# First-layer modulation matmuls: two weight loads to a run, placed first among the ready work

## The chip, the cores and the metric

The kernel runs on one core of a Trainium2 chip. A core has five engines with a queue each: TensorE (PE in the profile) for matmuls, VectorE (DVE), ScalarE (ACT), GpSimd (POOL), and SyncE (SP), which here issues nearly all transfers. Matmuls read SBUF and write PSUM banks of 128 partitions by 2 KB; a bank is free again when another engine has copied it out, which the text calls an evacuation. The metric is the time of one execution on the device in microseconds (us).

## The reference

The reference is a two-layer transformer backbone with 256 context tokens and 256 latent tokens, model width 2048. Each layer first makes shift, scale and gate vectors for the latent and the context stream from a condition vector; the normalised tokens are scaled and shifted by them, and only then go into the wide input projection:

```python
for l in range(DEPTH):                       # DEPTH = 2, D_MODEL = 2048
    shift, scale, gate = jnp.split(sc @ w_ada[l] + b_ada[l], 3, axis=-1)
    shift_c, scale_c, gate_c = jnp.split(sc_ctx @ w_ada[l] + b_ada[l], 3, axis=-1)
    h_lat = rms_norm(x, norm_g[l]) * (1.0 + scale[:, None]) + shift[:, None]
    h_ctx = rms_norm(xc, norm_g[l]) * (1.0 + scale_c) + shift_c
    lat_a, lat_b = mixer_inputs(h_lat, w_in[l], ...)      # h @ w_in, then q, k, v, gates
    ...
```

Two attention groups (grouped-query and latent-compressed), gates, an output projection and a gated residual follow, and after the second layer a final norm. The change touches only `sc @ w_ada[0]` and `sc_ctx @ w_ada[0]`, the shift and scale columns of them, in the first layer.

## The kernel before

Everything is float32. A projection product is made of three matmuls (L141, L142, L143, helper `mm3`): each operand is split into a rounded part `hi` (ScalarE, L114) and the rest `lo` (VectorE or GpSimd, L116), and hi x hi, lo x hi, hi x lo are summed into one of four `acc` banks of PSUM. VectorE evacuates a full bank by adding it onto a tile in SBUF (L449; L453 for the first time).

The first layer cannot project before its tokens are modulated, and the modulation needs 32 MB of `w_ada`. So `layer0` cuts the 16 blocks of 128 model columns into seven parts (block edges 0, 1, 2, 4, 6, 8, 12, 16, so parts 0 to 6 of 128, 128, 256, 256, 256, 512 and 512 columns). While the projections (`kv`, `cb`, `q`, `g` in the tile names) run over the model rows of one part, the sums of the next part are made between them. `ada_pe` does that for one part, as a generator: it loads the part's weights in loads of 1 MB (`ra` tiles, L210; two loads for 128 columns, four for 256, eight for 512; scale columns first, then shift) and multiplies 16, 8 or 4 slices of 128 rows per load with a stationary operand of 32 columns (`scp`, which holds the latent and the context vector). The matmuls L225 go in turn to four groups of 32 partitions of an `att` bank; L235 copies the bank, the small matmuls L239 add up the four groups and turn the result, and `ada_store` (L197, L199) writes scale and shift. Then `modulated` writes the tokens of the next part: per block and stream L359 on VectorE (`xT`), one ScalarE operation, and L361 on VectorE (`h`).

`wtile`, which loads and splits each projection weight, steps the generator (`bg_step`) five times per call in this stage, so each `yield` is a place where projection work comes between. Parts 0 and 1 load ahead of their first matmul. The `ra` tiles come from a pool of 14 buffers that holds much else; four or five of them are in turn at `ra`'s disposal, and a load waits on SyncE's queue until the matmuls that read its buffer before have run. The order of all instructions on each engine is fixed when the kernel is built: a scheduler simulates the program and takes, for each engine, the ready instruction of the highest priority; without other marks that goes by the order of the code.

Of the kernel before, what the change touches and what calls it, by code (L numbers as in the profile page):

```python
# [48 lines left out]
class Net:  # L49
# [151 lines left out]
    def ada_pe(self, l, c0, w, ahead=False):  # L201

        nc = self.nc
        n = 2048 // w
        at = [(kind, m) for kind in (1, 0) for m in range(0, KT, n)]

        def load(kind, m):
            r = self.blk("ra").rearrange("p (k n) -> p k n", k=n)
            wa = self.a["w_ada0"][m * P : (m + n) * P, kind * D + c0 : kind * D + c0 + w]
            self.ra = nc.sync.dma_start(out=r, in_=wa.rearrange("(k p) n -> p k n", p=P))  # L210
            return r

        rs = {}
        if ahead:
            rs = {z: load(*z) for z in at}
            yield

        ps = self.bank("att")[:, :w]
        for kind, m in at:
            r = rs[kind, m] if ahead else load(kind, m)  # L220
            for i in range(n):
                g = i % 4
                o = 2 if kind else 0
                with self.after(None if c0 else self.order):
                    nc.tensor.matmul(  # L225
                        ps[32 * g : 32 * g + 32, :],
                        lhsT=self.scp[:, m + i, o : o + 32],
                        rhs=r[:, i, :],
                        start=kind == 1 and m + i < 4,
                        stop=kind == 0 and m + i >= 12,  # L230
                    )
            if (kind, m) != at[-1]:
                yield
        part = self.tmp("part")[:, :w]
        nc.scalar.copy(part, ps)  # L235
        n = w // P
        f = self.bank("att")[:, : 4 * n].rearrange("p (k v) -> p k v", k=n)
        for i in range(n):
            nc.tensor.matmul(f[:, i, :], lhsT=part[:, i * P : (i + 1) * P], rhs=self.sel, start=True, stop=True)  # L239
        for kind in (1, 0):  # L240
            o = 0 if kind else 2
            self.ada_store(l, kind, f[:, :, o : o + 2], c0)
        yield
# [950 lines left out]
```

## Time and profile before

| | us |
|---|---|
| median of 3 runs | 1425.3 (1422.45 to 1426.04) |
| the profiled execution | 1427.46 |
| its span, first to last instruction | 1425.5 |
| TensorE busy | 1344.1 (94% of the span) |
| VectorE busy | 1092.9 (77%) |
| ScalarE busy | 602.6 (42%) |
| GpSimd busy | 404.0 (28%) |

The profiled execution lies 2.16 us above the median, and its own time is 1.96 us more than its span; a sum made from its rows stands against 1427.46. The mean granted clock of TensorE over the span is 0.983 of full speed. A number like 0.39 behind the start of a projection matmul is its own duration; matmuls overlap, so how fast they follow each other is read from their starts. A float32 matmul that is not split (L225, L239) leaves two records in the trace.

### The profile page before, as it was taken

To read this page: it belongs to the slowest core of one execution; us is meant where nothing else is said; L and a number is where in the kernel's file an instruction comes from. 1 tells how busy PE (TensorE), PEld (TensorE's weight loads), DVE (VectorE), ACT (ScalarE), POOL (GpSimd) and SP (SyncE) were. 2 spreads that over 40 slices of the span, in tenths; PEclk is the share of its full clock that TensorE was granted. 3 is DMA by queue.
4 is the path that set the end of the run, shared out by engine and by line. 5 is a ranking of instruction groups with operands and counts; after the bars stand their busy time and mean duration, and the time that the engine had idled before them with its cause. 6 is when DMAs were issued, how large, how long until landed. Compare 5 with 4: busy or idle time off the path is not lost.

```text
span 1425.5 us, 21028 instructions
## 1 busy us (share of the span) xinstructions
PE 1344.1 (94%) x7516; PEld 1128.2 (79%) x7516; DVE 1092.9 (77%) x2297; ACT 602.6 (42%) x974; POOL 404.0 (28%) x385
## 2 busy tenths in 40 slices
PE   5999999998998999898998999999999999999996
PEld 4765687887786987787886778898898989888884
DVE  2775568899796999988999864976787776856566
ACT  4321223544443242355532234665555644454443
POOL 0110025423222230222222113543234431223335
PEclk8999999999999999999999999999999999999999
DMA  9976733455555666443567665655775757733444
GB/s 307 349 262 223 284 113 89 144 166 166 159 175 179 205 213 211 151 139 126 190 216 220 214 208 184 203 150 177 234 256 163 234 153 249 260 110 126 156 137 143
DMA packets 142120, 272.47 MB, mean 191 GB/s; under 512 B 8336, under 2 KB 53824, under 8 KB 140608
## 3 DMA queue, kind: packets, MB, share of 16 engines
q1 hardware_dynamic: 142016, 271.13, 59.2%
q8 instruction: 59, 0.97, 0.3%
q14 instruction: 45, 0.37, 0.1%
HBM read 264.78 MB, written 6.32 MB: 190 GB/s over the span
## 4 chain that ended last, share of the span: by engine, by line
PE 59%; DVE 18%; DMA 12%; issue 5%; ACT 3%; POOL 2%; SPq 1%; DVEq 0%; POOLq 0%; ACTq 0%
PE acc L141 17%; PE acc L143 17%; PE acc L142 16%; DMA rad<-in_w_adaT 8%; DVE junk L269 7%; DVE lo L116 5%; PE att L225 2%; PE att L588 2%; PE att L611 1%; DMA cb<-in_cr 1%; DVE sm L593 1%; DMA ra<-in_w_ada 1%; DVE pt L148 1%; DMA raw<-in_w_in 1%; ACT p L596 1%
## 5 line engine op out<-in xcount | busy, mean ns | idle before, releaser
L114 ACT CAST hi<-raw 128x1024 fp32r<-128x1024 f32 (+2 forms) x279 | 271.8, 977 | 395.8 <-PE acc L142 224.2
L116 DVE TENSOR_TENSOR lo<-raw,hi 128x512 fp32r<-128x512 f32 (+2 forms) x446 | 305.6, 726 | 89.5 <-PE acc L143 37.5
L116 POOL TENSOR_TENSOR lo<-raw,hi 128x512 fp32r<-128x512 f32 (+2 forms) x112 | 153.7, 1393 | 476.5 <-PE acc L143 367.4
L141 PE MATMUL acc<-hi,h 128*128 128x512 f32 (+1 forms) x672 | 240.6, 361 | 6.1 <-ACT cq L451 4.9
L142 PE MATMUL acc<-hi,h 128*128 128x512 f32 (+1 forms) x672 | 238.1, 357 | 0.0
L269 DVE CUSTOM_DVE_ANT_0 junk<-rad,cb 128x512 bf16<-128x512 f32 x224 | 176.9, 790 | 73.5 <-DMA rad<-in_w_adaT 46.8
L143 PE MATMUL acc<-lo,h 128*128 128x512 f32 (+1 forms) x672 | 226.7, 359 | 3.0 <-DVE lo L116 2.3
L269 DVE CUSTOM_DVE_ANT_0 junk<-rad,cb,as 128x512 bf16<-128x512 f32 x224 | 190.3, 849 | 3.8
L142 PE MATMUL acc<-h,lo 128*128 128x512 f32 (+1 forms) x512 | 171.5, 340 | 2.7 <-DVE lo L116 2.6
L143 PE MATMUL acc<-h,hi 128*128 128x512 f32 (+1 forms) x512 | 170.0, 338 | 0.0
L141 PE MATMUL acc<-h,hi 128*128 128x512 f32 (+1 forms) x512 | 165.7, 343 | 1.9 <-DVE g L453 1.2
L599 POOL TENSOR_SCALAR p<-p,sm 128x512 f32<-128x512 f32 (+1 forms) x96 | 85.7, 898 | 284.9 <-DVE sm L597 249.3
L143 PE MATMUL acc<-lo,y 128*128 128x512 f32 x384 | 146.2, 400 | 9.7 <-DVE lo L116 8.7
L141 PE MATMUL acc<-hi,y 128*128 128x512 f32 x384 | 151.0, 398 | 2.3 <-ACT y L147 1.9
L141 PEld LDWEIGHTS acc<-hi,h 128*128 128x128 f32 x672 | 127.3, 189 | 32.8 <-issue 5.8
L142 PE MATMUL acc<-hi,y 128*128 128x512 f32 x384 | 151.7, 395 | 0.2 <-DVE y L148 0.2
L143 PEld LDWEIGHTS acc<-lo,h 128*128 128x128 f32 x672 | 124.5, 189 | 22.7 <-DVE lo L116 3.9
L142 PEld LDWEIGHTS acc<-hi,h 128*128 128x128 f32 x672 | 127.2, 189 | 15.4
L141 PEld LDWEIGHTS acc<-h,hi 128*128 128x128 f32 x512 | 93.6, 190 | 18.0 <-issue 2.1
L142 PEld LDWEIGHTS acc<-h,lo 128*128 128x128 f32 x512 | 96.9, 190 | 12.8 <-DVE lo L116 3.7
L143 PEld LDWEIGHTS acc<-h,hi 128*128 128x128 f32 x512 | 96.7, 190 | 9.8
L143 PEld LDWEIGHTS acc<-lo,y 128*128 128x128 f32 x384 | 73.1, 191 | 28.4 <-DVE lo L116 12.6
(219 smaller groups left out, 2292.2 us busy)
## 6 DMA issues: line engine op xcount, KB each, us to landing
rad<-in_w_adaT SPq DMA_DIRECT2D x128, 512.0 KB, 4.5
raw<-in_w_in SPq DMA_DIRECT2D x125, 512.0 KB, 4.4
raw<-in_w_out SPq DMA_DIRECT2D x72, 512.0 KB, 4.1
ra<-in_w_ada SPq DMA_DIRECT2D x32, 1024.0 KB, 8.7
raw<-in_w_in SPq DMA_DIRECT2D x48, 288.0 KB, 3.0
raw<-in_w_ukv SPq DMA_DIRECT2D x16, 512.0 KB, 3.4
cb<-in_cr SPq DMA_DIRECT2D x6, 1024.0 KB, 7.1
raw<-in_w_uq SPq DMA_DIRECT2D x12, 512.0 KB, 3.7
```

The lines of the kernel that those rows point to most:

```text
L114: nc.scalar.copy(h, t)
L116: e.tensor_tensor(out=lo[:, c], in0=t[:, c], in1=fr(h[:, c]), op=ALU.subtract)
L141: mm(out, lhsT=ah, rhs=bh, start=first, stop=False)
L142: mm(out, lhsT=al, rhs=bh, start=False, stop=False)
L143: return mm(out, lhsT=ah, rhs=bl, start=False, stop=last)
L148: self.nc.vector.tensor_tensor(out=lo, in0=src, in1=fr(hi), op=ALU.subtract)
L225: nc.tensor.matmul(ps[32 * g : 32 * g + 32, :], lhsT=self.scp[:, m + i, o : o + 32], rhs=r[:, i, :], start=kind == 1 and m + i < 4, stop=k ...
L269: nc.vector.tensor_tensor_reduce(out=junk, in0=r[:, cs], in1=cb[:, v, cs], scale=1.0, scalar=o if i else 0.0, op0=ALU.mult, op1=ALU.add, a ...
L588: self.order = nc.tensor.matmul(banks[j], lhsT=q[:, qs], rhs=k[:, ks], start=i == 0, stop=i == len(score) - 1)
L593: nc.vector.tensor_reduce(out=nb[:, c], in_=v, axis=AX.X, op=ALU.max)
L596: nc.scalar.activation(pr[j], banks[j], AF.Exp, bias=nb[:, j : j + 1], scale=sc[:, j : j + 1], accum_out=l[:, j : j + 1])
L599: nc.gpsimd.tensor_scalar(out=pr[j], in0=pr[j], scalar1=l[:, j : j + 1], scalar2=1.0, op0=ALU.mult, op1=ALU.mult)
```

## The change

`ada_pe` now groups its loads in twos (`runs`). Both loads of a pair are issued, then the matmuls of the second load and those of the first are written one behind the other, under `high_priority`, which puts them ahead of other ready work in the scheduler's choice; the `yield` stands behind the pair. The flags for the first and the last matmul of each group of partitions follow the new order. From here on the lines stand 4 higher (L225 is L229, L239 is L243, L449 is L453).

```diff
+        runs = [at[i : i + 2] for i in range(0, len(at), 2)]
         rs = {}
         if ahead:
             rs = {z: load(*z) for z in at}
             yield
 
         ps = self.bank("att")[:, :w]
-        for kind, m in at:
-            r = rs[kind, m] if ahead else load(kind, m)
-            for i in range(n):
-                g = i % 4
-                o = 2 if kind else 0
-                with self.after(None if c0 else self.order):
-                    nc.tensor.matmul(
-                        ps[32 * g : 32 * g + 32, :],
-                        lhsT=self.scp[:, m + i, o : o + 32],
-                        rhs=r[:, i, :],
-                        start=kind == 1 and m + i < 4,
-                        stop=kind == 0 and m + i >= 12,
-                    )
-            if (kind, m) != at[-1]:
+
+        for run in runs:
+            if not ahead:
+                rs = {z: load(*z) for z in run}
+            for j, (kind, m) in enumerate(run[::-1]):
+                for i in range(n):
+                    g = i % 4
+                    o = 2 if kind else 0
+                    with self.after(None if c0 else self.order), self.tc.high_priority():
+                        nc.tensor.matmul(
+                            ps[32 * g : 32 * g + 32, :],
+                            lhsT=self.scp[:, m + i, o : o + 32],
+                            rhs=rs[kind, m][:, i, :],
+                            start=run is runs[0] and j == 0 and i < 4,
+                            stop=run is runs[-1] and j == 1 and i >= n - 4,
+                        )
+            if run is not runs[-1]:
                 yield
```

The number of instructions on each engine stays the same. In the fixed order, past some 190 us of the trace of before, the instructions of every engine follow each other as before; GpSimd's order is unchanged throughout.

TensorE's queue in part 5, before (`att_1036` is the bank of its sums, `ra_...` a load, `acc_...` a projection's bank; 32x512 x2 is two matmuls of 32 columns by 512):

```order
L141 MATMUL acc_974<-hi_953,h_667 128x512
L142 MATMUL acc_974<-hi_953,h_668 128x512
L143 MATMUL acc_974<-lo_954,h_667 128x512
L225 MATMUL att_1036<-ra_1049,scp 32x512
L141 MATMUL acc_982<-hi_953,h_667 128x512
L142 MATMUL acc_982<-hi_953,h_668 128x512
L143 MATMUL acc_982<-lo_954,h_667 128x512
```

and the same projection weights (`hi_953`) in the order of the change:

```order
L141 MATMUL acc_958<-hi_953,h_667 128x512
L142 MATMUL acc_958<-hi_953,h_668 128x512
L143 MATMUL acc_958<-lo_954,h_667 128x512
L141 MATMUL acc_966<-hi_953,h_667 128x512
L142 MATMUL acc_966<-hi_953,h_668 128x512
L229 MATMUL att_1036<-ra_1051,scp 32x512 x4
L229 MATMUL att_1036<-ra_1049,scp 32x512 x4
L143 MATMUL acc_966<-lo_954,h_667 128x512
```

Where one matmul of a load stood alone between two projection products, all four of it now stand behind the four of the load that comes after it, eight in a row.

TensorE's queue at the start, before: the sums of parts 0 (`att_199`) and 1 (`att_260`) and the first projection.

```order
L225 MATMUL att_199<-ra_194,scp 32x128 x16
L225 MATMUL att_199<-ra_196,scp 32x128 x16
L239 MATMUL att_234<-k,part_232 128x4
L225 MATMUL att_260<-ra_248,scp 32x128 x16
L225 MATMUL att_260<-ra_250,scp 32x128 x16
L141 MATMUL acc_300<-hi_255,h_239 128x512
```

and in the change:

```order
L229 MATMUL att_199<-ra_196,scp 32x128 x16
L229 MATMUL att_199<-ra_194,scp 32x128 x16
L243 MATMUL att_234<-k,part_232 128x4
L229 MATMUL att_260<-ra_250,scp 32x128 x16
L229 MATMUL att_260<-ra_248,scp 32x128 x16
L141 MATMUL acc_300<-hi_255,h_239 128x512
```

The two loads of each part have changed places; `ra_248` is still loaded ahead of `ra_250`.

VectorE's queue where the modulation for part 5's blocks is written, before (`kv`, `cb` and `q` are the tiles that projections are evacuated into):

```order
L449 TENSOR_TENSOR kv_252<-acc_1091,kv_252 128x512
L116 TENSOR_TENSOR lo_1195<-raw_1192,hi_1194 128x512 x2
L449 TENSOR_TENSOR cb_326<-acc_1134,cb_326 128x512
L449 TENSOR_TENSOR cb_326<-acc_1142,cb_326 128x512
L449 TENSOR_TENSOR cb_326<-acc_1150,cb_326 128x512
L197 TENSOR_TENSOR mod_88<-att_1126,vec_86 128x8
L197 TENSOR_TENSOR mod_87<-att_1126,vec_86 128x8
L199 SCALAR_TENSOR_TENSOR mod_88<-mod_88,vec_86 128x8
L359 SCALAR_TENSOR_TENSOR xT_99<-xT_99,mod_88,rb 128x256
L449 TENSOR_TENSOR cb_326<-acc_1158,cb_326 128x512
L359 SCALAR_TENSOR_TENSOR xT_99<-xT_99,mod_88,rb 128x256 x7
L449 TENSOR_TENSOR q_55_354<-acc_1199,q_55_354 128x512
```

and in the change:

```order
L197 TENSOR_TENSOR mod_88<-att_1087,vec_86 128x8
L197 TENSOR_TENSOR mod_87<-att_1087,vec_86 128x8
L199 SCALAR_TENSOR_TENSOR mod_88<-mod_88,vec_86 128x8
L363 SCALAR_TENSOR_TENSOR xT_99<-xT_99,mod_88,rb 128x256
L453 TENSOR_TENSOR kv_252<-acc_1111,kv_252 128x512
L363 SCALAR_TENSOR_TENSOR xT_99<-xT_99,mod_88,rb 128x256 x7
L365 SCALAR_TENSOR_TENSOR h_1128<-xT_99,mod_87,h_1127 128x256
L453 TENSOR_TENSOR kv_252<-acc_1119,kv_252 128x512
L116 TENSOR_TENSOR lo_1195<-raw_1192,hi_1194 128x512 x2
L453 TENSOR_TENSOR cb_326<-acc_1160,cb_326 128x512
L365 SCALAR_TENSOR_TENSOR h_1128<-xT_99,mod_87,h_1127 128x256 x4
L453 TENSOR_TENSOR cb_326<-acc_1168,cb_326 128x512
```

The same twenty-odd operations have moved ahead of the evacuations of one `kv` and all four `cb` accumulators and of the two casts `lo_1195`.

## Rows read from the trace of the kernel before

**Rows 1.** The page: busy time of an engine; the chain that ended last.

```profile
PE 1344.1 (94%) x7516; PEld 1128.2 (79%) x7516; DVE 1092.9 (77%) x2297; ACT 602.6 (42%) x974; POOL 404.0 (28%) x385
...
PE 59%; DVE 18%; DMA 12%; issue 5%; ACT 3%; POOL 2%; SPq 1%; DVEq 0%; POOLq 0%; ACTq 0%
PE acc L141 17%; PE acc L143 17%; PE acc L142 16%; DMA rad<-in_w_adaT 8%; DVE junk L269 7%; DVE lo L116 5%; PE att L225 2%; PE att L588 2%; PE att L611 1%; DMA cb<-in_cr 1%; DVE sm L593 1%; DMA ra<-in_w_ada 1%; DVE pt L148 1%; DMA raw<-in_w_in 1%; ACT p L596 1%
```

**Rows 2.** Windows: length, each engine's busy us, granted clock, DMA share, GB/s.

```profile
28.00:32.00 4.00, 1.56 (x36) 1.03 (x26) 0.64 (x2) 0.12 (x1) 0.00 (x0) 0.50 1.13 340
...
38.00:50.00 12.00, 12.00 (x58) 9.64 (x60) 10.30 (x22) 7.48 (x15) 1.43 (x2) 1.00 1.09 361
60.00:80.00 20.00, 20.00 (x134) 13.90 (x133) 19.74 (x38) 8.02 (x13) 6.66 (x8) 1.00 1.09 360
...
140.00:160.00 20.00, 19.61 (x99) 13.23 (x98) 16.93 (x33) 4.48 (x9) 2.73 (x2) 1.00 0.60 219
```

**Rows 3.** Timeline, TensorE, 26 to 36 us: start, duration, [idle before it <-releaser].

```profile
27.60 1.94 PE L225 MATMUL att<-ra,scp 128*32 128x128 f32 x32 [1.41 <-DMA ra<-in_w_ada]
31.98 1.93 PE L225 MATMUL att<-ra,scp 128*32 128x128 f32 x32 [2.44 <-DMA ra<-in_w_ada]
...
35.29 0.63 PE L142 MATMUL acc<-hi,h 128*128 128x512 f32 x1
35.71 0.63 PE L141 MATMUL acc<-hi,h 128*128 128x512 f32 x1
```

**Rows 4.** L225's records in all; timeline of TensorE around some of its runs.

```profile
L225 PE MATMUL att<-ra,scp x448: 272/403/617, 23.5 to 175.9; 128*32 128x256 f32 x64, 128*32 128x128 f32 x43, 128*32 128x512 f32 x43
...
60.74 1.07 PE L225 MATMUL att<-ra,scp 128*32 128x256 f32 x16
...
82.22 0.39 PE L143 MATMUL acc<-lo,h 128*128 128x512 f32 x1
82.53 0.62 PE L225 MATMUL att<-ra,scp 128*32 128x256 f32 x2
...
83.42 0.39 PE L142 MATMUL acc<-hi,h 128*128 128x512 f32 x1
...
107.02 0.39 PE L142 MATMUL acc<-hi,h 128*128 128x512 f32 x1
107.24 0.39 PE L143 MATMUL acc<-lo,h 128*128 128x512 f32 x1
107.56 1.91 PE L225 MATMUL att<-ra,scp 128*32 128x512 f32 x12
...
109.74 0.40 PE L142 MATMUL acc<-hi,h 128*128 128x512 f32 x1
...
116.30 1.04 PE L225 MATMUL att<-ra,scp 128*32 128x512 f32 x2
...
178.39 0.95 PE L239 MATMUL att<-k,part 128*128 128x4 f32 x8
```

**Rows 5.** Timelines of VectorE, GpSimd and TensorE around the modulation of part 5.

```profile
136.22 1.28 DVE L116 TENSOR_TENSOR lo<-raw,hi 128x512 fp32r<-128x512 f32 x2
...
144.70 0.48 DVE L359 SCALAR_TENSOR_TENSOR xT<-xT,mod,rb 128x256 f32<-128x256 f32 x1
...
145.06 2.73 POOL L116 TENSOR_TENSOR lo<-raw,hi 128x512 fp32r<-128x512 f32 x2 [39.65 <-PE acc L143]
...
145.70 4.35 DVE L359 SCALAR_TENSOR_TENSOR xT<-xT,mod,rb 128x256 f32<-128x256 f32 x7
149.98 0.68 DVE L449 TENSOR_TENSOR q<-acc,q 128x512 f32<-128x512 f32 x1
150.58 1.26 DVE L361 SCALAR_TENSOR_TENSOR h<-xT,mod,h 128x256 fp32r<-128x256 f32 x3
...
150.71 0.50 PE L141 MATMUL acc<-h,hi 128*128 128x512 f32 x1 [0.39 <-DVE q L449]
```

**Rows 6.** Tile `ra`: issue to landing of its loads, all 32; then one issued at 61.87.

```profile
DMA to landing us min/median/max: 5.4/8.7/15.4
...
DMA to landing us min/median/max: 10.9/10.9/10.9
```

## The prediction

> **What bounds the kernel now.** I read the page's busy line and chain first. TensorE is busy 94% of the 1425.5 us span; the chain that ended last is 59% TensorE, 18% VectorE and 12% transfers, and 2% of it is the line that this change edits, L225 [rows 1]. Then I read the stage in which L225 runs (23 to 178 us) window by window: TensorE is busy 20.00 of 20 us from 60 to 80 us and 19.61 from 140 to 160 us, at full clock, 1.00 from 38 us on [rows 2]. So in this stage TensorE is the limit and time taken from its queue is time gained, unless a new wait takes it. The transfers are no limit of their own later on: their share falls from 1.09 to 0.60 [rows 2]. Third I read the runs of L225 one by one.
>
> **What one run of L225 costs.** A projection matmul starts 0.22 to 0.23 us after the one before it: 107.02, 107.24 [rows 4]; I take 0.2275. The cost of a run is the start of the second projection matmul behind it, less the start of the last one ahead of it, less two such steps. One matmul of 256 columns (two records, x2): 83.42 - 82.22 - 0.455 = 0.75 us. Six matmuls of 512 columns (x12): 109.74 - 107.24 - 0.455 = 2.05 us. The busy times tell what grows with the number: at 256 columns 0.62 us for one matmul and 1.07 us for eight; at 512 columns 1.04 us for one and 1.91 us for six [rows 4]. So up to four matmuls, which fill the four 32-column groups, go side by side in one round; a round takes about 0.43 us at 256 columns (0.45 between one round and two) and 0.86 us at 512 (0.87), and each run pays some 0.33 us on top (0.75 - 0.43; 2.05 - 2 x 0.86). A run of one matmul therefore costs as much as one of four.
>
> The row shows 0.33 us for going into and out of the 32-column form. The Trainium skill, TensorEngine Tiling (Array Packing), section Key Properties, says that a change of tiling mode drains the engine; this trace agrees, with that 0.33 us, and the sum does not need the rule.
>
> **Runs before and after.** In the trace the 448 records of L225 [rows 4] stand in 29 runs, in the order printed for the change in 15. Parts 0 to 2 of the stage (3 runs before and after) keep their matmuls together already. The others, in matmuls per run:
> - part 3 (256 columns): 8, 8, 8, 8 before: 4 x 0.33 + 8 rounds x 0.43 = 4.8 us;
> - part 4 (256): 8, 1, 3, 1, 2, 17: 6 x 0.33 + 11 x 0.43 = 6.7 us;
> - part 5 (512): 1, 6, 2, 1, 3, 1, 6, 3, 9: 9 x 0.33 + 13 x 0.86 = 14.1 us;
> - part 6 (512): 4, 4, 4, 4, 4, 4, 8: 7 x 0.33 + 8 x 0.86 = 9.2 us.
>
> Together 34.8 us. After the change each of these parts runs in pairs of loads: 2, 2, 4 and 4 runs, each 16 matmuls of 256 or 8 of 512 columns, 0.33 + 4 x 0.43 = 2.05 us. Twelve runs are 24.6 us. The term is **-10.2 us**: 4.6 from fourteen switches and 5.6 from part-filled rounds. All of it lies on TensorE where TensorE is full. The bound below is 9 us, if some of the new runs stand between two matmuls of one accumulator (the order has such places) and pay 0.1 us more.
>
> **The first pair.** Before, the matmuls of part 1's first load ran at 27.60 while the second load was still under way, and only the other half stood behind the wait for it, 31.98 to 33.9 [rows 3]. Now the second load's matmuls stand first, so both halves run after 31.98. This lays one half, 1.94 us, on the path. The clock was 0.50 in this stretch [rows 2], where projection matmuls step by 0.42 us (35.29, 35.71) [rows 3]; full clock came at about 38 us. If that moment stays, the work pushed behind it runs at twice the pace and half of the 1.94 us comes back: about **+0.9 us**. Bounds: 0 if full clock comes earlier because TensorE is busy without a gap from 32 us on, and 2.6 us if it comes later by as much as the extra wait makes it.
>
> What speaks against this piece first is the row: after 2.44 us without work TensorE runs at 1.2 GHz. The Trainium skill, TensorE: Matmul & The Clock Gate, section HAM oscillation — how this bites in real kernels, warns of the same thing, that bursts with transfer waits between them keep the engine on the low clock. By it the whole 1.94 us or somewhat more would stay; the sum would be 1 to 2 us higher.
>
> **VectorE at part 5.** When a part's sums are complete, VectorE makes the next tokens-times-scale tiles (L197, L199, eight L359, eight L361) in one queue with the evacuations (L449) that free TensorE's accumulators. Before, the seven L359 took 4.35 us, the evacuation behind them started at 149.98, and TensorE stood 0.39 us at 150.71 for it [rows 5]. In the new order part 5 is complete some 30 projection matmuls earlier, and its chain stands among five evacuations and two casts (L116). By the rows: 0.4 (L197, L199), 0.4 (first L359), 0.6, seven L359, one L361 0.42, 0.6, casts 1.2, 0.6, four L361 1.7, 0.6, three L361 1.26, 0.6 [rows 5]. The seven L359 are 2.8 us by the one that runs alone (0.48, next start 0.40 later) and 4.3 us beside GpSimd's casts (145.06, 2.73 us) [rows 5]. That is 11.2 to 12.7 us for five accumulators, which TensorE makes in 5 x 6 x 0.2275 = 6.8 us: 4.3 to 5.8 us behind. Before, the same reckoning up to the evacuation at 149.98 gives 6.3 - 2.7 = 3.6 us behind with 0.39 us of wait, so the other banks cover some 3.2 us. The wait becomes 1.1 to 2.6 us, 0.7 to 2.2 more than before. GpSimd's casts keep their place in the program and the chain comes earlier, so I take a value near the lower end, **+1.0 us**, with 0 to 3 as bounds, which also hold a smaller wait of this kind at other parts.
>
> **Loads and queues.** Two loads now go out together. A load lands 5.4 to 15.4 us after its issue, median 8.7 [rows 6]. The tightest pair, the last of part 6, gets buffers that the pair two before it frees; between stand 30 projection matmuls and one run, 6.8 + 2.05 = 8.9 us. The queue is far from full by then (share 0.60 between 140 and 160 us [rows 2]). I take nothing, with 0 to 1 us as range. On SyncE some projection weights now stand behind two or four more loads; shifted by the order, the nearest of them still lands some 2 us before its use, so nothing is added. GpSimd's order does not change.
>
> **Sum.** -10.2 + 0.9 + 1.0 = -8.3 us against the profiled execution's own 1427.46 us (span 1425.5): 1419.2. The median of the runs shown is 1425.3, 2.16 lower, so the forecast is **1417.0 us**. Behind about 190 us every engine's order is the same as before, and what the later waits hang on is issued by the same queues, so the shift should stay to the end.
>
> **Rivals.**
> - *VectorE and the first pair take their upper bounds.* -10.2 + 2.6 + 3 = -4.6: about 1420.7. For it: VectorE's queue is strictly in order and already made TensorE wait once. Against: the 0.39 us of that wait.
> - *The gain is absorbed later.* The chain has 18% of VectorE and 12% of transfers [rows 1]; if those stages go by something that does not move with the first 180 us, up to all of it is given back: 1421 to 1425. Against: their loads are issued when buffers come free, so they move too.
> - *The pairs' loads come late: slower.* One row has a load land 10.9 us after issue in a full queue [rows 6]; the second of a pair would come 3 us behind it (1 MB at some 350 GB/s), 13.9 us. The last four tight pairs have 11.0, 10.8, 9.2 and 8.9 us by the order, the third of them for its second load alone, which waits for no other: short by 2.9, 3.1, 1.7 and 5.0, together 12.7 us, and some 4 us at half clock behind such gaps, as behind the 2.44 us gap of [rows 3]: -8.3 + 16.7 = +8.4, about 1433.7. It decides once the second load takes over some 11 us. Against: the queue's share at that place.
> - *Nothing is paid back*: both new costs at nought, 1415.1, and 1413 if part 6's runs are cheaper still.
> - That the runs do not become whole is excluded by the order, which shows 15 of them.
>
> **How the numbers follow.** A measurement of this kernel tells about 0.3%, 4.3 us, from no change; faster is below 1421.0. Forecast with its own range 1415.5 to 1419.5: 0.64. Upper bounds, 1419.5 to 1421.5: 0.14, of which 0.11 counts as faster. Absorbed later: 0.11. Late loads: 0.05. Nothing paid back: 0.06. Faster 0.64 + 0.11 + 0.06 = 0.81, same 0.03 + 0.11 = 0.14, slower 0.05. The range 1413.0 to 1421.5 leaves out the absorbed and the late cases.
>
> **What would show it.** In the changed profile: 15 runs of the edited line (then L229), those of 512 columns with 16 records and 1.8 to 2.0 us; the last part's small matmuls (L239, then L243), which stand at 178.39 us before [rows 4], near 170 us; both halves of part 1 behind about 32 us and full clock by 38 us; a wait of TensorE for an evacuation (then L453) of 0.7 to 2.6 us near 137 to 141 us. Wrong would be: waits of TensorE for `ra` loads after 60 us; the shift of 8 us at 180 us smaller at 600 us; or a run of eight matmuls that costs well over 2.05 us.

## The result and the profile after

| | before | changed |
|---|---|---|
| median, us | 1425.38 (13 runs, 1420.05 to 1430.86) | 1417.29 (13 runs, 1410.09 to 1420.45) |
| profiled execution, us | 1427.46 | 1413.77 |
| its span, us | 1425.5 | 1412.0 |

The ratio is 0.9945, 95% interval 0.9931 to 0.9958: 8 us faster, where the forecast was 1417.0. The profiled execution of the changed kernel is one of its faster ones, 3.5 us below the median, so the difference of the two spans, 13.5 us, is not the gain.

The page of the changed kernel, to set beside [rows 1] (busy time; the chain that ended last):

```profile
span 1412.0 us, 21026 instructions
...
PE 1331.6 (94%) x7516; PEld 1128.1 (80%) x7516; DVE 1094.0 (77%) x2297; ACT 602.6 (43%) x974; POOL 404.0 (29%) x385
...
PE 55%; DVE 21%; DMA 11%; issue 6%; ACT 3%; POOL 2%; SPq 1%; DVEq 0%; POOLq 0%; ACTq 0%
```

TensorE does the same 7516 records in 12.5 us less busy time; VectorE and GpSimd do the same work in the same time. VectorE's share of the chain has grown from 18% to 21%.

To place the gain, take two projection matmuls that both kernels have: the first behind part 2's sums and one behind the last sums of the first layer. Timeline of TensorE, before:

```profile
53.51 0.50 PE L141 MATMUL acc<-hi,h 128*128 128x512 f32 x1
...
192.94 0.39 PE L142 MATMUL acc<-hi,h 128*128 128x512 f32 x1
```

The same two in the changed kernel:

```profile
52.56 0.50 PE L141 MATMUL acc<-hi,h 128*128 128x512 f32 x1
...
183.26 0.39 PE L142 MATMUL acc<-hi,h 128*128 128x512 f32 x1
```

The stretch between them took 139.43 us and takes 130.70 us: **-8.73 us**. The remaining 0.95 us of the 9.68 us at the second matmul was there already at the first, and most of what the profiled execution has beyond that comes behind 1100 us, where the order of work is the same (the lead of 10 us grows to 13). Both are taken up below.

The runs of the edited line number 15. Timeline of TensorE around one of them, and the small matmuls of the last part, in the changed kernel:

```profile
119.88 0.39 PE L143 MATMUL acc<-h,hi 128*128 128x512 f32 x1
120.20 1.92 PE L229 MATMUL att<-ra,scp 128*32 128x512 f32 x16
...
122.40 0.40 PE L142 MATMUL acc<-h,lo 128*128 128x512 f32 x1
...
166.89 0.95 PE L243 MATMUL att<-k,part 128*128 128x4 f32 x8
```

Reckoned as in the prediction, this run costs 122.40 - 119.88 - 0.455 = 2.06 us; before, six matmuls cost 2.05 [rows 4] and a single one of 512 columns 1.18 (that at 102.27 us). The twelve runs of parts 3 to 6 cost 24.9 us together (10 of them 2.06 or 2.07, the others 2.13 and 2.15, waits left out). The 26 runs of the kernel before come to 35.1 us by the same reckoning, but twice in part 6 a single projection matmul stands between two of them (at 166.31 and 174.16 us), and there the reckoning counts the same 0.20 us in both runs; without that they cost 34.7 us. So the runs give **-9.8 us**.

What TensorE waits for between 26 and 200 us in the changed kernel (us in total, times, longest):

```profile
PE att L229 <- DMA ra<-in_w_ada: 5.4, 1, 5.4
PE acc L141 <- DVE cb L453: 0.7, 1, 0.7
PE acc L141 <- DVE g L453: 0.6, 1, 0.6
```

and the two evacuation waits in the timeline:

```profile
64.22 0.47 PE L141 MATMUL acc<-hi,h 128*128 128x512 f32 x1 [0.62 <-DVE g L453]
...
139.56 0.50 PE L141 MATMUL acc<-hi,h 128*128 128x512 f32 x1 [0.66 <-DVE cb L453]
```

The wait near 150 us [rows 5] is gone, two others have come. No wait for an `ra` load stands behind 60 us. A wait costs more than the profile's idle time: that is counted from the end of a matmul 0.39 us long, while without the wait the next would have started 0.23 us behind its start, so 0.62 us of idle time is 0.78 us from start to start. Counted so, with the matmul behind each wait, the wait near 64 us costs 0.8 us, the one near 140 us with a third of 0.13 us at 141 us some 1.0 to 1.1, and the one before cost 0.6 to 0.7: **+1.2 us**. -9.8 + 1.2 = -8.6, and 0.1 us of the 8.73 is left to all else.

The small matmuls of the last part stand at 166.89 us, where the prediction had "near 170 us": in the order of the change they come 8 projection matmuls earlier, 1.8 us, and this execution had a lead of 0.95 us from the start.

### The profile page after: what moved, and what is told of

It reads as the page before. It is cut to its first block, busy times and chain, and to the rows that moved or that the text cites. A ratio compares the mean times of both kernels' runs of the same rounds, so it can differ in the third digit from the quotient of the medians.

```text
span 1412.0 us, 21026 instructions
## 1 busy us (share of the span) xinstructions
PE 1331.6 (94%) x7516; PEld 1128.1 (80%) x7516; DVE 1094.0 (77%) x2297; ACT 602.6 (43%) x974; POOL 404.0 (29%) x385
## 4 chain that ended last, share of the span: by engine, by line
PE 55%; DVE 21%; DMA 11%; issue 6%; ACT 3%; POOL 2%; SPq 1%; DVEq 0%; POOLq 0%; ACTq 0%
PE acc L143 16%; PE acc L141 16%; PE acc L142 15%; DVE junk L273 8%; DMA rad<-in_w_adaT 7%; DVE lo L116 5%; PE att L592 3%; PE att L229 2%; PE att L615 1%; DMA raw<-in_w_in 1%; DMA cb<-in_cr 1%; DVE sm L597 1%; DVE pt L148 1%; DMA ra<-in_w_ada 1%; ACT hi L114 1%
```

## The experiments

Two measures serve for all. One is the timed ratio to the kernel before, which tells some 0.2%, 3 us. The other is the **stretch**, the time in the trace between the two matmuls above: 139.43 us before, 130.70 in the changed kernel. It excludes the start and everything behind the first layer's sums, and it repeats well, as the second trace of the changed kernel shows first.

### The changed kernel again

No edit.

> The changed kernel once more, beside the two below. The size of the step: 1417.3 against about 1425, ratio 0.9945 within 0.002. Its profile is a second look at the start: if the moment of full clock is set by the run of 32 matmuls without a gap (theory C), it comes at 34 to 35 us again; if it varies from execution to execution, it may come anywhere between 34 and 38 us. At 190 us its TensorE should stand 8 to 10 us earlier than the kernel before did.

Measured: 1416.37 us (10 runs), ratio 0.9946, interval 0.9926 to 0.9966. The two matmuls in this execution:

```profile
54.31 0.50 PE L141 MATMUL acc<-hi,h 128*128 128x512 f32 x1
...
185.02 0.39 PE L142 MATMUL acc<-hi,h 128*128 128x512 f32 x1
```

The stretch is 130.71 us, 0.01 from the first trace. The start is not the same. The pair of part 1 and the first projection, first trace of the changed kernel:

```profile
31.31 3.63 PE L229 MATMUL att<-ra,scp 128*32 128x128 f32 x64 [5.43 <-DMA ra<-in_w_ada]
34.88 0.50 PE L141 MATMUL acc<-hi,h 128*128 128x512 f32 x1
```

and second trace:

```profile
32.15 3.64 PE L229 MATMUL att<-ra,scp 128*32 128x128 f32 x64 [5.95 <-DMA ra<-in_w_ada]
35.73 0.80 PE L141 MATMUL acc<-hi,h 128*128 128x512 f32 x1
36.32 0.63 PE L142 MATMUL acc<-hi,h 128*128 128x512 f32 x1
```

Windows from 32 to 38 us (the third number from the end is the granted clock), first trace:

```profile
32.00:36.00 4.00, 4.00 (x61) 3.26 (x54) 1.56 (x5) 2.10 (x4) 0.00 (x0) 0.65 1.08 359
36.00:38.00 2.00, 2.00 (x12) 1.67 (x11) 1.26 (x2) 0.82 (x2) 0.00 (x0) 1.00 1.10 347
```

and second trace:

```profile
32.00:36.00 4.00, 3.85 (x65) 3.26 (x66) 1.44 (x4) 1.94 (x4) 0.00 (x0) 0.50 1.07 362
36.00:38.00 2.00, 2.00 (x6) 1.59 (x7) 0.59 (x1) 0.18 (x1) 0.00 (x0) 0.57 1.11 350
```

The same run of 64 records without a gap, and full clock comes before 36 us once and shortly before 38 us the other time, as in the kernel before. So theory C falls: the moment differs from execution to execution with one and the same kernel. With the moment as in the kernel before, the thirteenth projection matmul starts at 39.64 us, before at 38.80: **+0.84 us**, for which the prediction had +0.9. At the matmul behind the sums this execution is 192.94 - 185.02 = 7.92 us ahead of the kernel before.

The other traces of this study bear this out. Where the pair of part 1 stands whole (five traces: the two of the changed kernel, pairs without first place, four loads to a run, no casts on GpSimd), full clock comes between 34.8 and 37.7 us and the thirteenth projection matmul starts at 37.89 to 39.64 us, 38.84 on average. Where the first load's matmuls stand first (six: the kernel before, single loads, the first load first in every pair, part 1's first load first, and twice part 1's first load first without casts), full clock comes between 34.7 and 37.9 us and that matmul starts at 37.15 to 38.80 us, 37.91 on average. The moment scatters alike in both, and the whole pair costs 0.9 us, with this scatter known to within some 0.9 us either way.

### One load to a run

```diff
-        runs = [at[i : i + 2] for i in range(0, len(at), 2)]
+        runs = [at[i : i + 1] for i in range(0, len(at))]
```

(with the flags as before)

> The matmuls keep first place among the ready work, but each load makes a run of its own and the first load stands first again: 27 runs (3 + 24) with the same 48 rounds of four as the changed kernel, which has 15. Theory A (a run costs 0.33 us of going in and out of the 32-column form, plus its rounds): 12 more runs, +4.0 us on TensorE up to 190 us against the changed kernel, about 1421.3 us, ratio to the kernel before 0.997. Theory B (what pays is the first place, by which a part's sums are complete earlier, and the number of runs is incidental): within 1 us of the changed kernel, 1417.3, ratio 0.994. Each single run by A: 1.19 us at either width.

Measured: 1419.65 us (12 runs), ratio 0.9963, interval 0.9948 to 0.9978; the stretch is 134.34 us, 3.64 more than in the changed kernel and 5.09 less than before. One of the runs in the timeline of TensorE:

```profile
103.88 0.39 PE L142 MATMUL acc<-hi,h 128*128 128x512 f32 x1
104.20 1.06 PE L229 MATMUL att<-ra,scp 128*32 128x512 f32 x8
...
105.53 0.39 PE L141 MATMUL acc<-hi,h 128*128 128x512 f32 x1
```

and its one wait for VectorE from 26 to 200 us (total, times, longest):

```profile
PE acc L141 <- DVE cb L453: 1.5, 1, 1.5
```

A run of four matmuls costs 105.53 - 103.88 - 0.455 = 1.20 us. The rounds are alike and the waits for VectorE nearly so (1.5 us here, 1.4 in the changed kernel), so the 3.64 us are twelve more runs, 0.30 us each: the price of the switch, measured apart from the rounds. Theory B, that the number of runs is incidental, would have had this kernel within 1 us. Against the kernel before, the runs of parts 3 to 6 cost 28.7 us instead of 34.7: full rounds and two switches fewer, 6.0 us where the prediction's prices give 6.3. So first place alone brings 5.1 of the stretch's 8.73 us, pairs the rest.

### Pairs without first place

```diff
-                    with self.after(None if c0 else self.order), self.tc.high_priority():
+                    with self.after(None if c0 else self.order):
```

> Pairs of loads are issued together and written second load first, but without first place among the ready work: 22 runs, of 16, 16; 7, 2, 3, 20; 1, 7, 1, 3, 1, 2, 1, 16; 8, 4, 4, 8, 8 matmuls in parts 3 to 6, 19 runs with 37 rounds at the widths of 256 and 512 columns. Theory A: 4.1 + 5.2 + 12.9 + 8.5 = 30.7 us against 34.8 before and 24.6 in the changed kernel, so 4 us faster than before and 6 slower than the changed kernel: about 1423, ratio 0.998. Theory B': if issuing two loads together is what pays, as fast as the changed kernel, 0.994.

Measured: 1423.06 us (10 runs), ratio 0.9995, interval 0.9981 to 1.0010; the stretch is 138.85 us, 0.6 less than before and 8.15 more than in the changed kernel. The runs of parts 3 to 6 cost 31.0 us, as expected (30.7). The rest is VectorE; TensorE's waits for other engines' results at projection matmuls from 26 to 200 us in this kernel:

```profile
PE acc L141 <- DVE cb L453: 2.2, 1, 2.2
PE acc L141 <- DVE g L453: 0.6, 1, 0.6
PE acc L141 <- ACT hi L114: 0.3, 1, 0.3
```

So writing pairs alone gives 3.7 us in the runs and loses most of it to later evacuations: of the 4 us that were expected against the kernel before, the stretch shows 0.6. First place is needed to keep the runs whole.

### The first load first, in every pair

```diff
-            for j, (kind, m) in enumerate(run[::-1]):
+            for j, (kind, m) in enumerate(run):
```

> The changed kernel in all but one point: within each pair the first load's matmuls stand first. The scheduler then takes each load as soon as it counts it as landed, and the fixed order has 27 runs as with single loads, although the loads are issued in pairs and have first place. Theory A: 12 more runs than the changed kernel, +3.5 to +4 us at 190 us, each run 1.20 us, as the single loads had it. Rival: issuing two loads at once is worth something by itself (earlier landings, fewer waits): within 1.5 us of the changed kernel at 190 us.

Measured: one time, 1416.46 us; the stretch is 132.68 us, 2.0 more than in the changed kernel, and the 24 runs of parts 3 to 6 cost 1.20 us each, but for one of 1.06 that stands directly at a group of L243. So the reversed order inside a pair is what makes the run whole, 27 runs in the trace without it and 15 with it: with first place the scheduler takes a load's matmuls as soon as it counts that load as landed, and only when the later load's matmuls stand first do the earlier ones come right behind. The twelve extra runs show here with less than the expected 3.5 us, because this order has no wait for VectorE at all in the stretch, where the changed kernel's waits cost 1.8 us. Not the issue of two loads at once but the place of the modulation among the evacuations gives that back. What the reversed order is worth in the whole time is not shown: one execution cannot tell 1416.5 from 1417.3 us.

### Part 1's first load first

```diff
-            for j, (kind, m) in enumerate(run[::-1]):
+            for j, (kind, m) in enumerate(run if ahead else run[::-1]):
```

> The changed kernel, but in parts 0 and 1 the first load's matmuls stand first, as before, so that half of part 1's sums run while its second load is under way. The prediction's term: one half (1.94 us at 1.2 GHz) leaves the path and half of it is given back at the clock, so 0.9 us faster than the changed kernel, 1416.4; full clock at about 38 us as before. Theory C (the whole run of 32 matmuls without a gap brings full clock some 3 us earlier, as the changed kernel's trace has it at 34.9 us): not faster, the twelfth projection matmul about 1 us later than in the changed kernel, 1418.3.

Measured: 1415.10 us (7 runs), ratio 0.9949, interval 0.9928 to 0.9970. The stretch is 129.61 us. Timeline of TensorE:

```profile
27.17 1.08 PE L229 MATMUL att<-ra,scp 128*32 128x128 f32 x32 [0.27 <-DMA ra<-in_w_ada]
31.56 1.67 PE L229 MATMUL att<-ra,scp 128*32 128x128 f32 x32 [3.31 <-DMA ra<-in_w_ada]
33.16 0.80 PE L141 MATMUL acc<-hi,h 128*128 128x512 f32 x1
```

and two windows (granted clock third from the end):

```profile
28.00:32.00 4.00, 0.69 (x28) 0.44 (x20) 1.18 (x3) 0.84 (x2) 0.00 (x0) 0.99 1.10 344
32.00:36.00 4.00, 4.00 (x32) 3.10 (x25) 1.45 (x4) 2.02 (x4) 0.00 (x0) 0.59 1.07 358
```

One half is off the path: the first projection starts 1.7 us earlier than in the first trace of the changed kernel, the thirteenth 0.6 us earlier, 37.27 against 37.89, and 2.4 us earlier than in the second trace. The stretch is shorter by 1.1 us, since the waits for VectorE are 0.4 us here: the order of the modulation's operations came out a little differently. The times resolve neither. This trace has a low clock at another place, too, full until just before 32 us and low from there: it was still full while TensorE was idle for 3.3 us up to 31.56, and fell behind that. One more sign that the moment differs from execution to execution.

### Four loads to a run

```diff
-        runs = [at[i : i + 2] for i in range(0, len(at), 2)]
+        runs = [at[i : i + 4] for i in range(0, len(at), 4)]
```

(with the flags for four)

> Runs over four loads at a time: 7 runs in all places but the start (parts 3 to 6: 1, 1, 2 and two that stand one behind the other), 8 in the whole trace instead of 15. Theory A: 7 switches fewer than the changed kernel, -2.4 us, about 1415. Rival (late loads): the four loads of a run need four of the four or five buffers at once, so those of the next run go out only when the run before it has ended; TensorE waits for them in front of a run by 2 us or more, and the time is 1418 or more, with a drop of the granted clock behind the wait.

Measured: 1429.36 us (10 runs), ratio 1.0029, interval 1.0009 to 1.0050; the stretch is 143.40 us. Timeline of TensorE:

```profile
154.67 3.64 PE L229 MATMUL att<-ra,scp 128*32 128x512 f32 x32
169.71 5.86 PE L229 MATMUL att<-ra,scp 128*32 128x512 f32 x32 [11.39 <-DMA ra<-in_w_ada]
```

the window around the second of them (granted clock 0.66):

```profile
160.00:180.00 20.00, 10.29 (x52) 5.03 (x53) 4.03 (x7) 3.72 (x4) 0.00 (x0) 0.66 1.02 376
```

and the waits for loads from 26 to 200 us, the one at the start among them:

```profile
PE att L229 <- DMA ra<-in_w_ada: 16.5, 3, 11.4
```

This is the prediction's slower rival. The last four loads are issued when the run before frees its buffers, 155.8 to 158.4 us; the first lands at 161.5, the fourth at 169.66, 13.9 us behind the first issue, and the run wants the fourth first. TensorE stands for 11.4 us and comes back at 1.2 GHz: the same run of 32 records takes 5.86 us instead of 3.64. Theory A's saving is there all the same: without that wait and the 2.2 us of the low clock, the runs of parts 3 to 6 cost 22.6 us, 2.3 less than in the changed kernel, for seven switches. With two loads the tightest one was issued at 150.37, landed at 157.67 and was used at 159.42: 1.75 us to spare.

### No casts on GpSimd in the first stage

```diff
-        e = nc.gpsimd if POOL_LO and self.nlo % POOL_LO == 0 else nc.vector
+        e = nc.gpsimd if POOL_LO and self.nlo % POOL_LO == 0 and not (self.start and self.bg_rate) else nc.vector
```

> The changed kernel, with the three casts of the first stage that GpSimd makes (2.8 us each for two halves) given to VectorE (1.29 us). Theory D (VectorE's two-input operations slow down beside GpSimd's cast, and this makes the new wait): the four L365 that took 3.73 us take 1.7 us, TensorE's wait of 0.66 us for the evacuation behind them goes, and so may the 0.62 us near 64 us; TensorE stands 0.5 to 1.3 us earlier at 190 us than in the changed kernel: some 1416.5. Rival E (the place of the modulation ahead of the evacuations makes the wait, whatever GpSimd does): the waits stay or grow by the 1.29 us that VectorE takes over, 1417 to 1419.

Timelines around the new wait in the changed kernel, VectorE:

```profile
129.61 2.86 DVE L363 SCALAR_TENSOR_TENSOR xT<-xT,mod,rb 128x256 f32<-128x256 f32 x7
...
135.18 3.73 DVE L365 SCALAR_TENSOR_TENSOR h<-xT,mod,h 128x256 fp32r<-128x256 f32 x4
```

and GpSimd:

```profile
135.81 2.81 POOL L116 TENSOR_TENSOR lo<-raw,hi 128x512 fp32r<-128x512 f32 x2 [33.92 <-DVE h L365]
```

The four L365 one by one (ns, shortest/median/longest):

```profile
L365 DVE SCALAR_TENSOR_TENSOR h<-xT,mod,h x4: 480/990/1520, 135.2 to 137.4; 128x256 fp32r<-128x256 f32 x4
```

VectorE at the same place in the experiment:

```profile
136.30 1.26 DVE L365 SCALAR_TENSOR_TENSOR h<-xT,mod,h 128x256 fp32r<-128x256 f32 x3
```

and all of TensorE's waits for VectorE from 26 to 200 us there:

```profile
PE acc L141 <- DVE g L453: 0.6, 1, 0.6
```

Measured: 1416.39 us (6 runs), ratio 0.9938, interval 0.9917 to 0.9959; the stretch is 129.86 us, 0.84 less than in the changed kernel. In the changed kernel two of the four L365 take 0.48 us, as each of the three does in the experiment; the two beside GpSimd's two casts (1.39 and 1.46 us) take 1.52 and 1.50 us, and each ends some 0.3 us behind one of the casts (137.20 and 138.62 us). That lays 2.1 us on VectorE's queue ahead of an evacuation of `cb`. An evacuation, which has one of its inputs in PSUM, is not slowed: beside the cast from 65.42 us one takes its usual 0.69 us (65.57 us). With the casts gone the wait for `cb` is gone, so theory D holds for it, with one reserve: VectorE's order came out a little differently, too. With part 1's first load first, two L365 are as slow (1.54 and 1.50 us) and the wait is 0.29 us; the order sets how much of the 2.1 us reaches TensorE. The wait of 0.62 us for `g` stays: that one comes from the place of four L363 ahead of the evacuation, as rival E had it. The Trainium skill, SBUF — State Buffer, section SBUF: two separate sides, states that VectorE and GpSimd share a pair of ports to SBUF, which one of them holds for a whole instruction while the other is blocked; a VectorE operation with two SBUF inputs is included where GpSimd's operation reads SBUF, as the cast does. The 1.52 and 1.50 us against 0.48 agree with it.

### Part 1's loads behind two, or three, projection weights

```diff
+        if c0 == P:
+            for _ in range(6):
+                yield
         rs = {}
```

(11 instead of 6 for three weights; part 1 no longer loads ahead, and in part 0 the first load's matmuls stand first)

> As with part 1's first load first, but part 1's two loads are issued behind the first two projection weights (2 x 256 KB, 0.7 us each), so that 24 projection matmuls stand in TensorE's queue ahead of part 1's sums. In the changed kernel TensorE sits idle for 5.43 us up to 31.3 us for part 1's second load. Theory F (this wait is on the path because nothing else is queued ahead): 24 projection matmuls, 5.5 us at full clock, move into it; the second load lands about 1.4 us later; TensorE stands 3 to 5 us earlier at 60 us: about 1413. Rival G (the start is bound by the transfers, which run without a gap up to 90 us, so what is gained at 35 us is waited for at a later load): gain at 35 us, gone by 100 us, 1416 to 1418.

> The same with part 1's loads behind three projection weights: 36 projection matmuls ahead of part 1's sums. Theory F: 8.2 us of projection work in the gap, which is more than it holds; 0 to 1 us better than with two weights, if the modulation of part 1, which comes later, does not make TensorE wait. Rival: part 1's tokens come late, TensorE waits for VectorE or ScalarE near 42 us and loses what it gained: 1 to 3 us worse than with two weights.

With two weights: 1414.22 us (6 runs), ratio 0.9928, interval 0.9909 to 0.9947. With three: 1416.08 us (6 runs), ratio 0.9947, interval 0.9930 to 0.9965. Timeline of TensorE with two:

```profile
29.22 1.58 PE L141 MATMUL acc<-hi,h 128*128 128x512 f32 x4 [1.51 <-ACT h L367]
...
36.49 1.95 PE L232 MATMUL att<-ra,scp 128*32 128x128 f32 x64
```

The first projection starts at 29.22 instead of 34.88, but at the matmul behind part 2's sums the lead over the first trace of the changed kernel is 1.66 us, and 1.14 behind the last sums; over the second trace, whose start was 1.75 us later, it is 3.4 and 2.9 us. Much of the 5.4 us wait is thus no loss that can be had back: the first projection itself still waits 1.5 us for its tokens (`h`), up to 29.22 us, and the work in the gap runs at 1.2 GHz, its matmuls 0.43 us apart, up to 33 us. Theory F's 3 to 5 us are not shown, and neither is rival G's loss of all by 100 us; how much stands, the times don't tell (0.9928 and 0.9945 have intervals that overlap). With three weights part 1's tokens come late, as the rival had it: TensorE waits a second time for `h`, 1.5 us at 45 us, and later 1.1 us for `kv`, at 72 us.

### Two of these together

Both without GpSimd's casts: with part 1's loads behind two weights, and with part 1's first load first, the latter in two sets of runs.

> Part 1's two loads behind two projection weights, and the first stage's casts on VectorE alone. By the parts: 0.7 to 1.7 us from the start and 0.7 to 0.8 us from the wait near 139 us, so 1.5 to 2.5 us earlier than the changed kernel at 190 us, and some 1415, ratio 0.993. If the two gains don't add (VectorE has 4 us more to do in the stage and becomes late elsewhere), 1417.

> Part 1's first load first, and the first stage's casts on VectorE alone. By the parts: 0.6 us from the start, 0.7 to 0.8 us from the wait near 139 us and perhaps 0.5 from the one near 64 us: 1.3 to 1.9 us earlier than the changed kernel at 190 us, some 1415.5.

> The last kernel (part 1's first load first, the first stage's casts on VectorE) once more. Its trace had TensorE only 1.2 us ahead of the changed kernel's second look at 190 us, while its timed ratio was 0.9912 against 0.9946. If the stage tells all, the ratio is 0.9935 to 0.994 now; if there is a further gain that the stage doesn't show, 0.991 again.

Measured: the first 1415.55 us, ratio 0.9940, interval 0.9918 to 0.9962, 2.3 us ahead of the changed kernel's first trace behind the last sums, as expected, and 4.1 ahead of its second. The second 1413.63 us, ratio 0.9912 (0.9888 to 0.9936), and in the next set 1415.66 us, 0.9954 (0.9937 to 0.9971): no further gain behind the first number. Its stretch, 131.29 and 131.45 us, is not shorter than the changed kernel's, since TensorE now waits for `kv` or `h` (1.5 or 1.4 us) and for `hi` (0.6) elsewhere. No kernel of this study is shown to beat the changed one.

## Why the prediction was right, step by step

- **The runs, -10.2 us**: -9.8 us, 34.7 before (34.8 worked out) and 24.9 after (24.6); 15 runs, each of eight matmuls 2.06 us. The two halves of the term have their own experiments: twelve switches more cost 3.6 us at equal rounds, seven fewer save 2.3, full rounds and two switches fewer save 6.0, and the cut runs without first place cost 31.0 us where 30.7 were worked out. The bound of 9 us, for runs between two matmuls of one accumulator, was not needed: two such runs (108.25 and 113.78 us) cost 2.06 us like the rest.
- **The first pair, +0.9 us**: 0.84 us between two executions whose full clock came at the same moment, and 0.9 between the averages of five and six traces, known to within some 0.9 us. In the profiled execution that was compared first it came 3 us earlier, and the piece looked like a gain of 0.9 us; the second trace shows that this was the execution, not the change. The bound "0 if full clock comes earlier because TensorE is busy without a gap" named a mechanism that the runs don't bear out. One reading was off: the prediction has TensorE at 1.2 GHz "after 2.44 us without work", but the run ahead of that gap took 1.94 us, as long as the one behind it (1.93) [rows 3]; the clock was low already before the gap.
- **VectorE at part 5, +1.0 us**: 1.2 us, but not quite as described. The wait for the part-5 chain is 0.66 us, near 139 us as said, where the working had 1.1 to 2.6; set against the wait that went, part 5 accounts for only some 0.4 us. The lower end was argued with GpSimd's casts keeping their place while the chain comes earlier, and the seven L363 did stay clear of the cast (2.86 us); but the cast then fell on the four L365, 3.73 us instead of 1.7, which the working had not seen. The other 0.8 us came near 64 us, where the prediction had only a bound for "other parts". A wait that was sized too large and one that was missed offset each other: that the sum of this term fits is luck.
- **Loads, nothing**: right, with 1.75 us to spare at the tightest. The slower rival's mechanism is real, loads that go out only when a run frees their buffers and a TensorE that comes back at half clock, but with two loads it is not reached; with four it decides.
- **The shift stays**: behind the sums the second trace has 7.9 us, the timed runs 8 us. Between single executions the lead drifts by several us later on, both ways, with no change in the order: the first trace is 9.7 us ahead of the kernel before at 193 us, 10.5 at 600 and 13.5 at the end, the second 7.9, 10.2 and 7.1. Part of that is again the clock: windows from 690 to 710 us, first and second trace of the changed kernel:

```profile
690.00:710.00 20.00, 19.03 (x99) 15.70 (x99) 19.89 (x42) 13.03 (x23) 5.25 (x4) 1.00 0.57 211
```

```profile
690.00:710.00 20.00, 18.14 (x87) 15.15 (x86) 19.62 (x39) 12.00 (x22) 5.26 (x4) 0.91 0.55 206
```

  Twelve records of TensorE fewer stand in the second. It is why the spans of two profiled executions, 13.5 us apart here, are no measure of a change of 8.
- The sum, -9.8 + 0.84 + 1.2 = -7.8, stands beside -7.9 in the trace of equal clock and -8.1 in the medians.

## What to carry to other kernels

Where small matmuls are threaded between large ones of another shape, count the runs and the rounds, not the matmuls: here a run of one cost as much as a run of four, and going in and out cost 0.3 us. Making runs whole needs two things from a scheduler that goes by readiness, first place and a reason not to start early (the later load's matmuls first); how long the runs may grow is set by the buffers, since a run of all the buffers leaves none to load into. To compare traces across executions, measure a stretch between two instructions that both have, behind the clock's first rise, and take two traces of one kernel.

## What the runs showed of the hardware that was not expected

- The moment at which the granted clock rose at the start differed by 3 us between two executions of one kernel (before 36 us, and shortly before 38 us), with the same work ahead of it; and in another kernel's execution the full clock lasted through 3.3 us of idle TensorE (28 to 32 us, 0.99) and fell behind it.
- A stretch of 130 us at full clock repeated within 0.01 us (130.70 and 130.71) between two executions of one kernel whose spans were 1412.0 and 1418.4 us.
- A wait of TensorE cost 0.16 us more, from start to start of the matmuls, than the profile's idle time says (0.78 for 0.62 us): a matmul lasts 0.39 us and the next starts 0.23 us behind its start.
- GpSimd's cast tripled the time of the VectorE operation with two SBUF inputs beside it, 1.5 us for 0.48; an evacuation, with one input in PSUM, took its usual 0.69 us beside one.
